# Moving intermediates of two delta-rule mixers from SBUF to PSUM, two copies' engine and one subtraction's place

## The chip, the cores and the metric

The program runs on one core of a Trainium2 chip. The time is that of the whole program in device microseconds (us), the median of three runs. One core has five engines that run side by side, each through its own list of instructions in order: TensorE (PE, matrix products), VectorE (DVE), ScalarE (ACT), GpSimd (POOL) and SyncE (SP, which here only issues DMAs).

## The reference

Two blocks of a sequence model are applied to 512 tokens of 1024 features. The first block has two layers; each is a mixer and a feed-forward part. The change touches the two mixers of this block alone. What they compute, cut to the parts that matter:

```python
qkv = jax.nn.silu(centred_depthwise_conv(jnp.concatenate([qd, kd, vd], axis=-1), dn_conv_w[l]))  # 5 taps
qd = l2norm(qd...) * DN_DK ** -0.5 ; kd = l2norm(kd...)
...
gcum = jnp.cumsum(g, axis=-1)                      # g: log decay; chunks of 64 tokens, 8 heads
decay = jnp.exp(jnp.where(incl, gcum[..., :, None] - gcum[..., None, :], -jnp.inf))
a_kk = jnp.where(strict, jnp.einsum("bhnid,bhnjd->bhnij", k_beta, k) * decay, 0.0)
t_inv = lax.linalg.triangular_solve(eye + a_kk, ...)           # 64x64 unit lower triangles
qk = jnp.einsum("bhnid,bhnjd->bhnij", q, k) * decay
q_dec = q * jnp.exp(gcum)[..., None]
...
def step(state, inp): ...                          # a scan over the 8 chunks, both directions
```

Beside this delta rule each mixer has a softmax attention over the same tokens (queries and keys normalised per head and turned by a rotary table), and gates that mix the two branches.

## The kernel before

The activations lie in SBUF with features on partitions: a tile is 128 features x 512 tokens, one PSUM bank. A projection is 8 pieces of contraction times three matmuls of 512 columns (high x high, high x low, low x high parts of float32), 24 matmuls; the weights come by DMA (`wraw`, issued by SP), are rounded to a high part by ACT (`whi`, line 478), and POOL subtracts to get the low part (`wlo`, line 384, which is the line of a helper `tt` and so of most two-tensor operations).

A mixer (`_mix`) runs in this order. First come eight tiles of keys and queries, each through `conv_tile`: a projection, a product with the row norms into `pad` (line 384), ACT's first tap (line 701), four taps of DVE (line 703) and a SiLU (lines 516 and 517). `l2` normalises them: squares, transposes and sums, a Newton root on DVE (lines 394 to 400), the roots spread into `rce` (line 453, in `spread`), transposed on PE and multiplied into the tiles (line 733). Then `inside` goes through four pairs of heads and two directions, eight steps. A step takes two exponentials on ACT (lines 847 and 853) and on DVE and POOL: the decayed keys (line 849, `s<-kq,eg`), the decayed queries (POOL, `s<-kq,eg`), a subtraction (POOL), a minimum with the mask (DVE, `x<-x,cstt`), the product with the query-key matrix (DVE, `s<-kkqq,x`), the one with beta (POOL) and the one with the key-key matrix (DVE, `x<-x,kkqq`). The results go to DRAM. Beside `inside` run `vproj` (four convolution tiles of values, `cv`) and `zproj` (four tiles `z`). After that the key-key matrices are read back as `N`, and `solve` inverts all triangles on DVE: for j = 1 to 30 a product into `ntmp` and a sum into `N`. Beside the solve run the attention's keys and queries and some gates; `core`, the attention itself, starts before the solve has ended: scores (line 955), maxima (line 959), exponentials, transposes, the two parts `pT` and `pTl`, and the product with the values (line 974) into a bank from `psg`. Last come the scan over the chunks and the output projections.

PSUM has eight banks. Two are always kept for projections (`psb`); `self.banks(3, 3)` gives the first stage of a mixer three of kind `pss` and three of kind `psf`; the solve and the attention have `banks(2, 3, 1)`, one of them of kind `psg`. A buffer of a pool is given again only when the last use of what it held is over.

The order of each engine's list is set by a scheduler, which goes by its own simulated times; generators with costs (`side.beside(inside(), R1)`) only set the order in which the program is written.

Of the kernel before, what the change touches and what calls it, by code (L numbers as in the profile page):

```python
# [305 lines left out]
class Prog:  # L306
# [139 lines left out]
    def spread(self, rc, wide=None, nt=4, psum=None):  # L446


        nc = self.nc
        if wide is not None:  # L450
            e = self.nrm.tile([P, 4, P], F32, name="rce", tag="nsq", bufs=2)
            for a, b in wide(e, rc):
                nc.vector.tensor_copy(a, b)
            col = lambda t: e[:, t]
        else:
            col = lambda t: rc[:, t].broadcast_to((P, P))
        ps = (psum or self.pss)()
        for t in range(nt):
            nc.tensor.transpose(ps[:, t * P:(t + 1) * P], col(t), self.ident)
        return ps  # L460
# [187 lines left out]
    def _mix(self, l, nm, nxt, mp):  # L648
# [30 lines left out]
        mt = mid.enter_context(tc.tile_pool(name="mid", bufs=1))  # L679
        th = lambda name="th", bufs=3: mt.tile([P, S], F32, name=name, tag=name, bufs=bufs)  # L680
        bk = ExitStack()
        bk.enter_context(self.banks(3, 3))
        reg = ExitStack()
        r1 = reg.enter_context(tc.tile_pool(name="mr1", bufs=1))
        cs = lambda name, bufs=2, shape=(P, S): r1.tile(list(shape), F32, name=name, tag=name, bufs=bufs)
# [5 lines left out]
        npad = [0]  # L691


        def conv_tile(i, w, c):
            ps = self.psb()
            self.proj(ps, w, nm.acts)
            u = pads[npad[0] % 2]
            npad[0] += 1
            self.tt(u[:, 2:S + 2], ps, nm.r, ALU.mult)
            tap = lambda k: self.vec(f"cw{l}", i * 5 + k)  # L700
            nc.scalar.activation(c, u[:, 2:S + 2], AF.Copy, scale=tap(2))
            for k in (0, 1, 3, 4):
                nc.vector.scalar_tensor_tensor(c, u[:, k:k + S], tap(k), c, ALU.mult, ALU.add)
            return c

        kq = []

        def qk_pair(g, first, a):
            ws = self.wload(win[g], 8, 256)
            for j in range(2):  # L710
                if a == 0:
                    kq.append(kv("kq", (first + j) // 2))
                c = kq[first + j][:, a]
                conv_tile(first + j + 4 * (1 - a), ws[j], c)
                self.silu2(c, c, th())


        wide2 = lambda e, a: [(e.rearrange("p t (h d) -> p t h d", h=2), a.unsqueeze(3).broadcast_to((P, 4, 2, 64)))]
# [92 lines left out]
        def vproj():  # L811
            for g in range(4, 6):
                ws = self.wload(win[g], 8, 256)
                for j in range(2):
                    p = 2 * (g - 4) + j
                    c = conv_tile(8 + p, ws[j], th("cv", 2))
                    t = th()
                    self.silu2(c, c, t)
                    by_chunk(vst[:, :, p], c, self.psf(), 0.5)
                    yield 6  # L820

# [4 lines left out]
        def inside():  # L826
            for p in range(4):
                kT, qT = kq[p][:, 0], kq[p][:, 1]
                kb, km = kbds[p % 2], kkqq[p % 2].rearrange("p a (c k x) -> p (a c) k x", c=4, k=2)
                for h in range(2):  # L830
                    sl = slice(h * 64, h * 64 + 64)
                    nc.scalar.copy(kb[sl, :, sl], c8(kT)[sl])
                for b in range(2):
                    ps = self.pss()
                    for c in range(4):
                        sl = slice((4 * b + c) * 64, (4 * b + c) * 64 + 64)
                        nc.tensor.matmul(ps[:, c * P:(c + 1) * P], kb[:, 4 * b + c], kq[p][:, :, sl], start=True, stop=True)
                    nc.scalar.copy(kkqq[p % 2][:, b], ps)
                kk, qq = km[:, :, 0], km[:, :, 1]
                kt = cs("kt")  # L840
                by_chunk(c8(kt), kT, self.pss(), 1.0)
                nc.sync.dma_start(out=scrK[:, p].rearrange("q c x -> q (c x)"), in_=kt)
                for d in (1, 0):
                    u0 = (d * 4 + p) * 8
                    gr = grs[2 * p + 1 - d]
                    eg = cs("eg")
                    nc.scalar.activation(eg, gr, AF.Exp)
                    s3 = cs("s3", 2, (P, 3, S))
                    nc.vector.scalar_tensor_tensor(s3[:, KE], kT, -1.0, eg, ALU.mult, ALU.mult)
                    self.tt(s3[:, QD], qT, eg, ALU.mult, "gpsimd")  # L850
                    self.tt(c8(gr), c8(gr), gc[:, u0:u0 + 8].unsqueeze(2).broadcast_to((P, 8, 64)), ALU.subtract, "gpsimd")
                    self.tt(c8(gr), c8(gr), mask[d].unsqueeze(1).broadcast_to((P, 8, 64)), ALU.min)
                    nc.scalar.activation(gr, gr, AF.Exp)
                    self.tt(c8(s3[:, QK]), qq, c8(gr), ALU.mult)
                    for h, a in enumerate(half):
                        nc.sync.dma_start(out=dn[d, a, p, 0:h + 2:h + 1].rearrange("q k c x -> q k (c x)"), in_=s3[a, 0:2])
                        nc.sync.dma_start(out=dn[d, half[1 - h], p, 1 + h].rearrange("q c x -> q (c x)"), in_=s3[a, QK])
                    self.tt(c8(gr), c8(gr), nbeta[:, u0:u0 + 8].unsqueeze(2).broadcast_to((P, 8, 64)), ALU.mult, "gpsimd")
                    self.tt(c8(gr), c8(gr), kk, ALU.mult)
                    if d == 0:  # L860
                        nc.sync.dma_start(out=scrN[:, p].rearrange("c q x -> q c x"), in_=c8(gr))
                    else:
                        ps = self.pss()
                        for t in range(4):
                            nc.tensor.transpose(ps[:, t * P:(t + 1) * P], gr[:, t * P:(t + 1) * P], self.ident)
                        nt = cs("nt")
                        nc.scalar.copy(nt, ps)
                        for c2 in range(2):
                            nc.sync.dma_start(out=scrT[:, c2:8:2, p], in_=nt[c2 * 64:c2 * 64 + 64].rearrange("i (t y) -> i t y", t=4))
                    yield 8  # L870
# [46 lines left out]
        def queries(g):  # L917
# [7 lines left out]
            rq[g] = self.rs_cols([sq for _, sq in qs], four, 2, 1.0, 64 * EPS, psum=self.psf, r=nm)  # L925
            for q, _ in qs:
                turn(q)
                for h in range(2):
                    t = at.tile([P, S], F32R, name="qa", tag="qa", bufs=5)
                    qa.append(t)  # L930
                    nc.scalar.copy(t, q)
                    for o in (0, 64):
                        a, b = slice(o + h * 32, o + h * 32 + 32), slice(o + 32 - h * 32, o + 64 - h * 32)
                        self.tt(t[b], q[a], t[a].bitcast(F32), ALU.subtract, "gpsimd")
            yield 2

        pv_last = []
# [78 lines left out]


        def solve(sp):
            tmp = sp.tile([P, 1024], F32, name="ntmp")
            Nm = N[:, :4096].rearrange("p (j i) -> p j i", j=64)  # L1020
            nc.sync.dma_start(out=Nm[64:128], in_=scrT.rearrange("j c p (h i) -> (c p h) j i", h=2))
            nc.sync.dma_start(out=Nm[0:64], in_=scrN.rearrange("c p (h j) i -> (c p h) j i", h=2))
# [2 lines left out]
            Nh = N.rearrange("p (a x) -> p a x", a=2)[:, :, :2048].rearrange("p a (j i) -> p a j i", i=64)  # L1025
            for j in range(1, 31):
                n = 31 - j
                t = tmp[:, :2 * j * n].rearrange("p (a c i) -> p a c i", a=2, c=j)
                self.tt(t, Nh[:, :, 0:j, j:j + 1].broadcast_to((P, 2, j, n)),
                        Nh[:, :, j:j + 1, j + 1:32].broadcast_to((P, 2, j, n)), ALU.mult)  # L1030
                self.tt(Nh[:, :, 0:j, j + 1:32], Nh[:, :, 0:j, j + 1:32], t, ALU.add)
# [771 lines left out]
```

## Time and profile before

| | |
|---|---|
| median of 3 runs | 3408.35 us (3406.65 to 3415.18) |
| the profiled execution | 3408.12 us, span from first to last instruction 3406.3 us |
| PE busy | 3214.2 us, 94% of the span |
| DVE, POOL, ACT busy | 1917.2 us (56%), 1810.2 us (53%), 1486.5 us (44%) |

A busy share is a mean over the whole program. The two mixers lie near 13 to 490 us and 936 to 1365 us, the rest is feed-forward parts, and another block. A row of a view has the line of the program, the engine, the operation, the tile written and the tiles read, the shapes, and times.

### The profile page before, as it was taken

How to read it: one execution, taken by the hardware profiler on the slowest of the kernel's cores; microseconds unless marked ns; L12 is line 12 of the kernel's file. 1: busy time of each engine (PE TensorE's matmuls, PEld its weight loads, DVE VectorE, ACT ScalarE, POOL GpSimd, SP SyncE). 2: the span in 40 equal slices, each digit the busy share in tenths (PEclk: the TensorE clock that was granted, in tenths of full speed). 3: DMA queues.
4: the chain of work that ended last, by engine and by line, in shares of the span. 5: the costliest groups of instructions: out<-in, count | busy, mean ns of one | idle time of the engine just before them, and what ended most of it. 6: DMA issues, size and time to landing. Idle time of an engine off the chain costs nothing. (4 is left out here: it accounts for less than half of the span.)

```text
span 3406.3 us, 46975 instructions
## 1 busy us (share of the span) xinstructions
PE 3214.2 (94%) x17342; PEld 2649.1 (78%) x17342; DVE 1917.2 (56%) x3561; ACT 1486.5 (44%) x2776; POOL 1810.2 (53%) x1493
## 2 busy tenths in 40 slices
PE   8878899999987889999999998999999999999999
PEld 6667778888776667788887787878888888888887
DVE  8988555554698866573455665463223666453222
ACT  4636434343554553443343335544334455544332
POOL 4653465444565434654455556555556335655554
PEclk9989999999998999999999999999999999999999
DMA  4532532222354234322232213233223213222222
GB/s 145 166 90 62 132 117 99 96 90 96 122 155 126 71 92 132 133 93 94 99 113 75 75 47 127 87 125 122 95 99 108 82 65 118 99 87 99 99 99 87
DMA packets 140477, 350.93 MB, mean 103 GB/s; under 512 B 43567, under 2 KB 80815, under 8 KB 111576
## 3 DMA queue, kind: packets, MB, share of 16 engines
q1 hardware_dynamic: 138816, 344.44, 31.4%
q10 hardware_dynamic: 1432, 3.49, 0.4%
q8 instruction: 138, 2.26, 0.3%
q14 instruction: 91, 0.75, 0.1%
HBM read 316.34 MB, written 34.16 MB: 103 GB/s over the span
## 5 line engine op out<-in xcount | busy, mean ns | idle before, releaser
L384 POOL TENSOR_TENSOR wlo<-wraw,whi 128x512 fp32r<-128x512 f32 (+2 forms) x1044 | 1372.0, 1318 | 1363.9 <-ACT whi L478 1333.9
L478 ACT CAST whi<-wraw 128x512 fp32r<-128x512 f32 (+2 forms) x1044 | 631.6, 608 | 1111.7 <-PE psb L494 846.6
L491 PE MATMUL psb<-act,whi 128*128 128x512 f32 x1888 | 756.6, 401 | 50.8 <-DVE x L384 15.5
L494 PE MATMUL psb<-act,whi 128*128 128x512 f32 x1888 | 750.8, 398 | 0.6 <-DVE act L277 0.6
L495 PE MATMUL psb<-act,wlo 128*128 128x512 f32 x1888 | 749.3, 398 | 1.7 <-POOL wlo L384 1.6
L491 PEld LDWEIGHTS psb<-act,whi 128*128 128x128 f32 x1888 | 361.9, 192 | 130.3 <-issue 34.1
L495 PEld LDWEIGHTS psb<-act,wlo 128*128 128x128 f32 x1888 | 361.4, 191 | 79.1 <-POOL wlo L384 3.7
L494 PEld LDWEIGHTS psb<-act,whi 128*128 128x128 f32 x1888 | 361.9, 192 | 74.4 <-DVE act L277 2.0
L384 DVE TENSOR_TENSOR x<-psb,x 128x512 f32<-128x512 f32 x168 | 115.2, 689 | 381.3 <-PE psb L495 381.0
L491 PE MATMUL ps<-act,whi 128*128 128x512 f32 (+1 forms) x720 | 282.5, 392 | 3.4 <-ACT rB L303 3.4
L494 PE MATMUL ps<-act,whi 128*128 128x512 f32 (+1 forms) x720 | 281.6, 391 | 0.0
L495 PE MATMUL ps<-act,wlo 128*128 128x512 f32 (+1 forms) x720 | 281.6, 391 | 0.0
L491 PE MATMUL psb<-mid,whi 128*128 128x512 f32 x704 | 276.7, 394 | 1.0 <-DVE x L384 1.0
L495 PE MATMUL psb<-mid,wlo 128*128 128x512 f32 x704 | 276.2, 392 | 0.0
L494 PE MATMUL psb<-mid,whi 128*128 128x512 f32 x704 | 273.6, 389 | 0.0
L491 PEld LDWEIGHTS ps<-act,whi 128*128 128x128 f32 (+1 forms) x720 | 134.9, 187 | 34.4 <-ACT rB L303 4.9
L495 PEld LDWEIGHTS ps<-act,wlo 128*128 128x128 f32 (+1 forms) x720 | 134.7, 187 | 29.9
L494 PEld LDWEIGHTS ps<-act,whi 128*128 128x128 f32 (+1 forms) x720 | 135.0, 188 | 29.4
L495 PEld LDWEIGHTS psb<-mid,wlo 128*128 128x128 f32 x704 | 132.2, 188 | 30.5
L494 PEld LDWEIGHTS psb<-mid,whi 128*128 128x128 f32 x704 | 132.1, 188 | 29.5
L491 PEld LDWEIGHTS psb<-mid,whi 128*128 128x128 f32 x704 | 132.3, 188 | 29.3 <-DVE x L384 1.5
L384 DVE TENSOR_TENSOR cv<-ps,cv 128x512 f32<-128x512 f32 (+1 forms) x60 | 41.5, 692 | 174.6 <-PE ps L495 106.8
(434 smaller groups left out, 5584.8 us busy)
## 6 DMA issues: line engine op xcount, KB each, us to landing
wraw<-in_wup SPq DMA_DIRECT2D x44, 1024.0 KB, 4.8
wraw<-in_fup SPq DMA_DIRECT2D x44, 1024.0 KB, 4.8
wraw<-in_win SPq DMA_DIRECT2D x38, 1024.0 KB, 5.0
wraw<-in_wdn SPq DMA_DIRECT2D x16, 1024.0 KB, 4.8
wraw<-in_evin SPq DMA_DIRECT2D x16, 1024.0 KB, 4.8
wraw<-in_xakv SPq DMA_DIRECT2D x16, 1024.0 KB, 4.8
wraw<-in_fdn SPq DMA_DIRECT2D x16, 1024.0 KB, 4.8
wraw<-in_odin SPq DMA_DIRECT2D x12, 1024.0 KB, 4.9
```

What stands on the lines that cost most here:

```text
L384: getattr(self.nc, eng).tensor_tensor(out, a, b, op)
L478: nc.scalar.copy(hi, part)
L491: mm = nc.tensor.matmul(ps, hi[:, i], acts[k][:, 0, :n], start=k == 0, stop=False)
L494: nc.tensor.matmul(ps, hi[:, i], acts[k][:, 1, :n], start=False, stop=False)
L495: nc.tensor.matmul(ps, lo[:, i], acts[k][:, 0, :n], start=False, stop=k == kc - 1)
```

## The change

Five edits, all in the two mixers:

- the four DVE taps of `conv_tile` accumulate in a PSUM bank (`psg`), and the SiLU's last operation writes the result to SBUF; the first stage's banks become `(2, 2, 2)`;
- both exponentials of an `inside` step are written to PSUM banks of kind `psf` (`eg`, `en`); the decayed queries move from POOL to DVE; beta is multiplied into the key-key matrix (`kb`, still POOL) ahead of the decay instead of after it;
- the copies that spread roots (`rce`) go from DVE to ACT;
- in `queries`, POOL's four subtractions of 32 partitions for each pair of heads' low parts, eight for each of the two groups of queries, become one of 128 partitions to `lo`, followed by four DMAs on SP;
- the solve's product goes to a PSUM bank `pt`, the one bank of kind `psg`, instead of SBUF; `ntmp` stays for a later layout step.

```diff
@@ spread
-                nc.vector.tensor_copy(a, b)
+                nc.scalar.copy(a, b)
@@ _mix
-        bk.enter_context(self.banks(3, 3))
+        bk.enter_context(self.banks(2, 2, 2))
@@ conv_tile
-        def conv_tile(i, w, c):
-            ps = self.psb()
+        def conv_tile(i, w, out):
+            ps, c = self.psb(), self.psg()
...
                 nc.vector.scalar_tensor_tensor(c, u[:, k:k + S], tap(k), c, ALU.mult, ALU.add)
-            return c
+            self.silu2(c, out, th())
@@ inside
-                    eg = cs("eg")
+                    eg = self.psf()
                     nc.scalar.activation(eg, gr, AF.Exp)
                     s3 = cs("s3", 2, (P, 3, S))
                     nc.vector.scalar_tensor_tensor(s3[:, KE], kT, -1.0, eg, ALU.mult, ALU.mult)
-                    self.tt(s3[:, QD], qT, eg, ALU.mult, "gpsimd")
+                    self.tt(s3[:, QD], qT, eg, ALU.mult)
...
-                    nc.scalar.activation(gr, gr, AF.Exp)
-                    self.tt(c8(s3[:, QK]), qq, c8(gr), ALU.mult)
+                    en = self.psf()
+                    nc.scalar.activation(en, gr, AF.Exp)
+                    self.tt(c8(s3[:, QK]), qq, c8(en), ALU.mult)
...
-                    self.tt(c8(gr), c8(gr), nbeta[:, u0:u0 + 8].unsqueeze(2).broadcast_to((P, 8, 64)), ALU.mult, "gpsimd")
-                    self.tt(c8(gr), c8(gr), kk, ALU.mult)
+                    kb = cs("eg")
+                    self.tt(c8(kb), kk, nbeta[:, u0:u0 + 8].unsqueeze(2).broadcast_to((P, 8, 64)), ALU.mult, "gpsimd")
+                    self.tt(c8(gr), c8(en), c8(kb), ALU.mult)
@@ queries
+                lo = th("cv", 2)
+                self.tt(lo, q, ts[0].bitcast(F32), ALU.subtract, "gpsimd")
+                for h, t in enumerate(ts):
                     for o in (0, 64):
                         a, b = slice(o + h * 32, o + h * 32 + 32), slice(o + 32 - h * 32, o + 64 - h * 32)
-                        self.tt(t[b], q[a], t[a].bitcast(F32), ALU.subtract, "gpsimd")
+                        nc.sync.dma_start(out=t[b].bitcast(F32), in_=lo[a])
@@ solve
-            tmp = sp.tile([P, 1024], F32, name="ntmp")
+            tmp, pt = sp.tile([P, 1024], F32, name="ntmp"), self.psg()
...
-                t = tmp[:, :2 * j * n].rearrange("p (a c i) -> p a c i", a=2, c=j)
+                t = pt[:, :2 * j * n].rearrange("p (a c i) -> p a c i", a=2, c=j)
```

The lists move at three places. The first is DVE's list where `inside` begins in the first mixer. Before, the first decayed keys (`s_881`, `s_967`) stand among the convolution taps and ahead of the second normalisation, whose sums begin at the last row:

```order
L453 COPY rce<-rc 128x512
L703 SCALAR_TENSOR_TENSOR cv<-pad_227,vect,cv 128x512
L849 SCALAR_TENSOR_TENSOR s_881<-kq,eg 128x512
L849 SCALAR_TENSOR_TENSOR s_967<-kq,eg 128x512
L384 TENSOR_TENSOR pad_228<-psb,rB 128x512
L703 SCALAR_TENSOR_TENSOR cv<-pad_228,vect,cv 128x512
L733 SCALAR_TENSOR_TENSOR kq<-kq,ps_587 128x512
L733 SCALAR_TENSOR_TENSOR kq<-kq,ps_595 128x512
L703 SCALAR_TENSOR_TENSOR cv<-pad_228,vect,cv 128x512
L384 TENSOR_TENSOR x<-x,cstt 128x512
L420 TENSOR_REDUCE sums<-ps_779 128x8
```

Now the same place in the program has all taps (`ps_1173` is the last convolution's bank) and the whole second normalisation in front; the first decayed keys are `s_889`:

```order
L703 SCALAR_TENSOR_TENSOR ps_1173<-pad_228,vect,ps_1173 128x512
L398 SCALAR_TENSOR_TENSOR rsq<-rsq,ps_811 128x32
L384 TENSOR_TENSOR rsq<-rsq,ps_811 128x32
L400 SCALAR_TENSOR_TENSOR rc<-rsq,ps_811 128x32
L731 SCALAR_TENSOR_TENSOR kq<-kq,ps_832 128x512
L731 SCALAR_TENSOR_TENSOR kq<-kq,ps_840 128x512
L731 SCALAR_TENSOR_TENSOR kq<-kq,ps_848 128x512
L731 SCALAR_TENSOR_TENSOR kq<-kq,ps_856 128x512
L846 SCALAR_TENSOR_TENSOR s_889<-kq,ps_887 128x512
L384 TENSOR_TENSOR s_889<-kq,ps_887 128x512
L384 TENSOR_TENSOR x<-x,cstt 128x512
```

The eight steps of `inside` have moved behind the second normalisation, whose banks are of the same kind as theirs.

The second place is the end of the solve on DVE in the first mixer. Before, six values of `pTl` stand further ahead among the solve's sums (not shown), and the seventh behind the last sum:

```order
L384 TENSOR_TENSOR N<-N,ntmp 128x2x29x2
L384 TENSOR_TENSOR ntmp<-N 128x60
L959 TENSOR_REDUCE mx<-ps_2253 128x1
L384 TENSOR_TENSOR N<-N,ntmp 128x2x30
L384 TENSOR_TENSOR mx<-mx,rc 128x1
L1042 COPY ntmp<-N 64x1024
L384 TENSOR_TENSOR pTl<-ps_2118,pT 128x4x128
L959 TENSOR_REDUCE mx<-ps_2268 128x1
```

Now, with `ps_1520` the bank of the products and `ps_1943` the first bank of the attention's output:

```order
L384 TENSOR_TENSOR ps_1520<-N 128x60
L384 TENSOR_TENSOR mx<-mx,rc 128x1 x2
L384 TENSOR_TENSOR N<-N,ps_1520 128x2x30
L1044 COPY ntmp<-N 64x1024
L384 TENSOR_TENSOR pTl<-ps_2083,pT 128x4x128
L384 TENSOR_TENSOR pTl<-ps_2126,pT 128x4x128
L384 TENSOR_TENSOR cv<-ps_1943,cv 64x512
L1045 COPY N<-N 64x32x32
L384 TENSOR_TENSOR pTl<-ps_2151,pT 128x4x128
L384 TENSOR_TENSOR pTl<-ps_2166,pT 128x4x128
```

Only four values of `pTl` now stand ahead of the last sum, and the next ones and the first output of the attention (`cv<-ps_1943`) follow behind it.

The third place is SP's list between the reading of `N` and the writing of the inverses (`ti`). Before:

```order
L1022 DMA N<-scrN 64x4096
L1021 DMA N<-scrT 64x64x64
L465 DMA wraw<-in_win 128x2048 x6
L1048 DMA ti_196<-N 16x4096
```

Now:

```order
L1024 DMA N<-scrN 64x4096
L868 DMA scrT<-nt 256x1x128 x2
L1023 DMA N<-scrT 64x64x64
L465 DMA wraw<-in_win 128x2048 x2
L936 DMA qa<-cv 32x512 x4
L465 DMA wraw<-in_win 128x2048
L936 DMA qa<-cv 32x512 x4
L465 DMA wraw<-in_win 128x2048 x2
```

Three of the weight fetches stand behind DMAs that wait for POOL's `lo` (in a tile named `cv`).

## Rows read from the trace of the kernel before

**Rows 1.** Busy time by stretch: first mixer thrice, a feed-forward part, second mixer's solve.

```profile
core 0: us, PE busy (x) PEld busy (x) DVE busy (x) ACT busy (x) POOL busy (x), PEclk, DMA share, GB/s
29.00:167.40 138.40, 120.03 (x616) 97.00 (x617) 130.44 (x176) 76.09 (x144) 82.05 (x56) 0.96 0.48 141
186.30:267.60 81.30, 68.20 (x296) 55.06 (x297) 79.68 (x136) 31.99 (x63) 42.80 (x28) 0.90 0.19 67
267.60:345.00 77.40, 65.94 (x372) 52.20 (x372) 61.37 (x116) 50.02 (x102) 28.17 (x20) 1.00 0.22 55
595.00:680.00 85.00, 85.00 (x375) 70.06 (x375) 44.08 (x48) 31.96 (x52) 42.09 (x32) 1.00 0.26 92
1064.50:1145.10 80.60, 68.92 (x296) 55.60 (x297) 79.44 (x136) 32.03 (x63) 42.37 (x28) 0.88 0.20 70
```

**Rows 2.** Timeline near 148 us, DVE and POOL: start, us, engine, line.

```profile
146.78 3.41 POOL L384 TENSOR_TENSOR wlo<-wraw,whi 128x512 fp32r<-128x512 f32 x2
147.29 1.75 DVE L703 SCALAR_TENSOR_TENSOR cv<-pad,vect,cv 128x512 f32<-128x512 f32 x1
148.97 1.77 DVE L384 TENSOR_TENSOR x<-x,kkqq 128x512 f32<-128x512 f32 x1
```

**Rows 3.** Instructions on tile pad: count, shortest/median/longest ns, first and last start.

```profile
L384 DVE TENSOR_TENSOR pad<-psb,rB x112: 675/686/694, 29.0 to 3363.8; 128x512 f32<-128x512 f32 x112
L703 DVE SCALAR_TENSOR_TENSOR kq<-pad,vect,kq x64: 730/752/1830, 30.5 to 965.1; 128x512 f32<-128x512 f32 x64
```

**Rows 4.** Groups of instructions by line and form: busy us, mean ns, idle before.

```profile
L703 DVE SCALAR_TENSOR_TENSOR kq<-pad,vect,kq 128x512 f32<-128x512 f32 x64 | 63.8, 1010 | 5.9 <-ACT kq L701 5.3
L384 POOL TENSOR_TENSOR qa<-th,qa 32x512 fp32r<-32x512 f32 x32 | 47.7, 1492 | 9.4 <-ACT qa L931 4.0 <-issue 3.6
L703 DVE SCALAR_TENSOR_TENSOR cv<-pad,vect,cv 128x512 f32<-128x512 f32 x32 | 33.2, 1041 | 2.1 <-ACT cv L701 1.6
L849 DVE SCALAR_TENSOR_TENSOR s<-kq,eg 128x512 f32<-128x512 f32 x16 | 26.8, 1694 | 0.0
L384 DVE TENSOR_TENSOR x<-x,kkqq 128x512 f32<-128x512 f32 x16 | 24.1, 1528 | 0.0
L384 DVE TENSOR_TENSOR x<-x,cstt 128x512 f32<-128x512 f32 x16 | 15.9, 997 | 2.6 <-POOL x L384 2.6
L453 DVE COPY rce<-rc 128x512 f32<-128x512 f32 x16 | 12.9, 825 | 0.0
L847 ACT ACTIVATE eg<-x 128x512 f32<-128x512 f32 x16 | 10.1, 632 | 28.8 <-POOL s L384 11.0 <-DVE s L849 10.6 <-DMA x<-scrG 5.0
```

**Rows 5.** Instructions on tile kq, two of DVE's, in the columns of rows 3.

```profile
L517 DVE SCALAR_TENSOR_TENSOR kq<-th,kq x16: 673/692/1692, 38.5 to 966.6; 128x512 f32<-128x512 f32 x16
L733 DVE SCALAR_TENSOR_TENSOR kq<-kq,ps x16: 672/675/680, 89.9 to 1014.4; 128x512 f32<-128x512 f32 x16
```

**Rows 6.** Timeline of DVE: first decayed keys, second normalisation's copies, last key-key products.

```profile
93.99 1.76 DVE L849 SCALAR_TENSOR_TENSOR s<-kq,eg 128x512 f32<-128x512 f32 x1
...
123.43 2.45 DVE L453 COPY rce<-rc 128x512 f32<-128x512 f32 x2
...
165.03 2.37 DVE L384 TENSOR_TENSOR x<-x,kkqq 128x512 f32<-128x512 f32 x2
```

**Rows 7.** The solve's two groups, all forms together, in both mixers.

```profile
L384 DVE TENSOR_TENSOR ntmp<-N 128x60 f32<-128x60 f32 (+14 forms) x60 | 49.3, 822 | 16.2 <-DMA N<-scrT 15.4
L384 DVE TENSOR_TENSOR N<-N,ntmp 128x60 f32<-128x60 f32 (+14 forms) x60 | 40.7, 679 | 0.5
```

**Rows 8.** Two of the solve's fifteen sizes by themselves, both mixers.

```profile
L384 DVE TENSOR_TENSOR N<-N,ntmp 128x440 f32<-128x440 f32 x4 | 2.4, 611 | 0.1
L384 DVE TENSOR_TENSOR N<-N,ntmp 128x60 f32<-128x60 f32 x4 | 0.9, 232 | 0.0
```

**Rows 9.** What PE waited for: total us, times, longest.

```profile
PE psb L491 <- DVE N L384: 12.0, 2, 6.3
PE psb L491 <- ACT whi L478: 9.8, 1, 9.8
PE ps L955 <- DVE rc L384: 7.2, 2, 3.6
```

**Rows 10.** A DMA issue of SP from 80 to 200 us: count, size, us to landing.

```profile
dnscr<-s SPq DMA_DIRECT2D x16, 128.0 KB, 4.7
```

More of the change, by code (lines that the diff above doesn't have):

```diff
@@ L712, in qk_pair @@
                     kq.append(kv("kq", (first + j) // 2))
-                c = kq[first + j][:, a]
-                conv_tile(first + j + 4 * (1 - a), ws[j], c)
-                self.silu2(c, c, th())
+                conv_tile(first + j + 4 * (1 - a), ws[j], kq[first + j][:, a])
         wide2 = lambda e, a: [(e.rearrange("p t (h d) -> p t h d", h=2), a.unsqueeze(3).broadcast_to((P, 4, 2, 64)))]
@@ L815, in vproj @@
                     p = 2 * (g - 4) + j
-                    c = conv_tile(8 + p, ws[j], th("cv", 2))
-                    t = th()
-                    self.silu2(c, c, t)
+                    c = th("cv", 2)
+                    conv_tile(8 + p, ws[j], c)
                     by_chunk(vst[:, :, p], c, self.psf(), 0.5)
@@ L828, in inside @@
                 kT, qT = kq[p][:, 0], kq[p][:, 1]
-                kb, km = kbds[p % 2], kkqq[p % 2].rearrange("p a (c k x) -> p (a c) k x", c=4, k=2)
+                kbd, km = kbds[p % 2], kkqq[p % 2].rearrange("p a (c k x) -> p (a c) k x", c=4, k=2)
                 for h in range(2):
                     sl = slice(h * 64, h * 64 + 64)
-                    nc.scalar.copy(kb[sl, :, sl], c8(kT)[sl])
+                    nc.scalar.copy(kbd[sl, :, sl], c8(kT)[sl])
                 for b in range(2):
@@ L836, in inside @@
                         sl = slice((4 * b + c) * 64, (4 * b + c) * 64 + 64)
-                        nc.tensor.matmul(ps[:, c * P:(c + 1) * P], kb[:, 4 * b + c], kq[p][:, :, sl], start=True, stop=True)
+                        nc.tensor.matmul(ps[:, c * P:(c + 1) * P], kbd[:, 4 * b + c], kq[p][:, :, sl], start=True, stop=True)
                     nc.scalar.copy(kkqq[p % 2][:, b], ps)
@@ L927, in queries @@
                 turn(q)
-                for h in range(2):
-                    t = at.tile([P, S], F32R, name="qa", tag="qa", bufs=5)
-                    qa.append(t)
+                ts = [at.tile([P, S], F32R, name="qa", tag="qa", bufs=5) for h in range(2)]
+                qa.extend(ts)
+                for t in ts:
                     nc.scalar.copy(t, q)
+                lo = th("cv", 2)
+                self.tt(lo, q, ts[0].bitcast(F32), ALU.subtract, "gpsimd")
+                for h, t in enumerate(ts):
                     for o in (0, 64):
                         a, b = slice(o + h * 32, o + h * 32 + 32), slice(o + 32 - h * 32, o + 64 - h * 32)
-                        self.tt(t[b], q[a], t[a].bitcast(F32), ALU.subtract, "gpsimd")
+                        nc.sync.dma_start(out=t[b].bitcast(F32), in_=lo[a])
             yield 2
```

## Prediction

> **What bounds the kernel now.** I read the busy time by stretch first. In a feed-forward part PE is busy all of 85 us and issues 375 matmuls, one every 0.227 us [rows 1]; nothing that the other engines do faster can help there, and the change does not touch it. The mixers are different. From 29.0 to 167.4 us, the convolutions and `inside`, DVE is busy 130.4 of 138.4 us; from 186.3 to 267.6, the solve, 79.7 of 81.3, and in the second mixer the solve's stretch looks the same [rows 1]. The granted clock there is 0.96 and 0.90; PE stands still in between. So DVE sets the pace of these two stretches, and what it saves there can be seen in the end. Between them lies a DMA round trip, behind them the attention, where DVE has 61.4 of 77.4 us [rows 1] and nothing is saturated.
>
> The timeline tells why DVE is so full. Near 148 us one operation with two SBUF inputs takes 1.75 us, the next 1.77, while POOL works without a gap [rows 2]. The same tap elsewhere takes 0.730 at least and 0.752 in the middle, 1.830 at most; the product `pad<-psb,rB`, which reads one input from PSUM, runs 0.675 to 0.694 in all 112 cases [rows 3]. A DVE operation with both inputs in SBUF waits for POOL, one with an input in PSUM does not.
>
> **The change part by part**, for one mixer (rows that cover both are halved).
>
> Taps: 96 take 97.0 us [rows 4]. At 0.752 they take 72.2, so 12.4 us less per mixer. The decayed keys: 16 at 1.694; at 0.675, what `kq<-kq,ps` takes [rows 5], 8.0 less. The decayed queries come to DVE: eight at 0.675, 5.4 more. The key-key products: 1.528 to 0.675, 6.8 less. The eight copies of roots, 0.825 each, leave: 6.6 less [rows 4]; ACT, busy 76.1 of 138.4 us, has room for eight at about 0.63. Together DVE has 28 us less of its 130.
>
> No row shows an operation that writes 512 columns to PSUM and reads them back. Both ends: the row with PSUM input costs 0.675 against 0.673 for the shortest with SBUF alone [rows 5], so nothing; or the 0.079 us by which a tap exceeds it [rows 3, 5], on 122 operations of a mixer (48 taps, 12 SiLUs, 32 in `inside`, 30 sums) 9.6 us. I take nothing, since only the first row differs in the memory alone. [...]
>
> But the 28 us don't all shorten the stretch, because of the order. The two exponentials of a step now need banks of kind `psf`, which the second normalisation and `by_chunk` use as well; the order shows all eight steps behind that normalisation, where four decayed keys stood ahead of its root. So I place two points. The second normalisation's copies start at 123.4 us now [rows 6]. Of DVE's work ahead of them, 40 taps lose 10.3 us, the first copies leave 3.3, and four decayed keys, four minima, four query-key products (0.675 each) and two key-key products move behind, by rows 4 about 16.5: DVE would be there at 93.3. PE has 312 projection matmuls from 29.0 to that point, 70.8 us at 0.227, so not before 99.8; with 64 small transposes and the wait for the first normalisation I take 108. From there run eight steps. A step in which each waits for the one before is two exponentials at 0.632 [rows 4], four DVE operations at 0.675 and a minimum at 0.997, 4.96 us, and about one of a convolution's or `z`'s operations: 6.0. Eight end at 156, where 167.4 stands now (165.03 and 2.37 [rows 6]): 11 us earlier. The bounds of a step are 4.7, DVE's work alone, and 9.2, the pace now ((167.4 - 93.99) / 8): from 21 earlier to 14 later.
>
> The stretch of the round trip, 18.9 us to 186.3, I leave as it is.
>
> The solve: 60 sums take 40.7 us, 60 products 49.3 [rows 7]. From sizes 60 and 440 at 0.232 and 0.611 [rows 8] an operation alone is 0.172 us plus 0.997 per thousand elements; a solve has 30 sums with 9,920 elements, 15.1 us against 20.35: 5.3 less. The products still read both inputs from SBUF; only their output is in PSUM. I count no direct gain for them; bounds are 0 and 9.6 less. POOL has less to do: of its 42.8 us in this stretch [rows 1] eight of the 32-partition subtractions at 1.49 [rows 4] go, 11.9, and two of about 1.3 come. That is 22% less work of POOL's; of the 9.6 us that the products wait, 2.1 go. One copy of roots and one of sums go to ACT, 0.9. Together 8 us less, on an engine that stands idle for 1.6 us in this stretch: 8 us.
>
> [...] No row here shows an operation with two SBUF inputs and PSUM output. [...]
>
> What comes back: the solve's product holds the only `psg` bank, which the attention's output needs. Now six of 32 score tiles are through `pTl` before the solve's last sum; in the new order four are, and no product with the values. The next stretch takes 77.4 / 26 = 3.0 us a tile. Two tiles later at half that price, since their scores and maxima are done, is 3 us; bounds 0 and 6.
>
> The DMAs: sixteen per mixer on SP, each landing about 4.7 us after issue if it is like a 128 KB store [rows 10]. With 1.3 for the subtraction that is 6.0, where four of POOL's took 4 x 1.49 = 6.0. I cost them at nothing: PE waits at the scores for the root `rc`, not for `qa` [rows 9]. Weight fetches stand behind them on SP, but PE waited for weights only once, at the start [rows 9]; with that cover gone, one late fetch costs about a landing, 4.7 us.
>
> The 6 us twice that PE waited behind DVE's wait for `N` [rows 9] go, as `cv<-psb` now stands ahead of it; PE was not the pace there, so nothing.
>
> Sum for a mixer: 11 + 8 - 3 = 16; for both 32. From the profiled execution's 3408.1 us (span 3406.3 and 1.8 around it; it equals the median of 3408.35 within 0.3): 3376.
>
> **The rivals.** First, DVE's saving lands nearly whole: steps at 4.7 us and products relieved too. Then 21 + 8 + 8 - 3 = 34 a mixer, 3340 (the products' 9.6 less the 2.1 counted already are the second 8). For it: filler operations can cover the exponentials. Against it: the banks' order.
>
> Second, slower: two `psf` banks for `eg`, `en`, the values' transposes and, before them, the roots make each step wait for the release of the one before, and ACT, in order, holds exponentials behind weight rounding. At today's 9.2 us a step, `inside` ends 14 later: 14 - 8 + 3 = 9 a mixer, 3426. It decides from 8.1 us a step, where 108 + 8 x 8.1 = 173 eats the solve's 5 net.
>
> Third, given back: behind the solve, attention needs all six tiles again at 3.0 us, 18, so 11 + 8 - 18 = 1 a mixer, 3406. For it: PE and the chain of score, exponential and transpose set that stretch, not DVE. Against: maxima are taken ahead as before.
>
> Fourth, the change doesn't do what it says: reading and writing PSUM costs the 0.079 us, 9.6 a mixer. 16 - 9.6 = 6.4, 3395.
>
> **How the numbers follow.** Forecast 0.50, first rival 0.17, second 0.12, third 0.15, fourth 0.06. The forecast's own range is 3364 to 3387 (steps of 5.3 to 6.7 us). 8 in 10 reach from 3340 to 3408: below lies half of the first rival, above the second. A measurement tells about 0.3%, 10 us, from no change. Faster by more (below 3398): 0.48 of the forecast, 0.17 and 0.04 of the fourth, 0.69. Within: 0.02 of the forecast, 0.01 of the second, 0.13 of the third, 0.02 of the fourth, 0.18. Slower: 0.11 of the second and 0.02 of the third, 0.13.
>
> **What would show it.** Taps near 0.75 us in every case and no more of 1.75; decayed keys near 0.7; sums of the solve near 15 us a mixer, products still uneven; the last key-key product near 156; a solve stretch near 73 us; the first product with the values right behind the last sum; PE's clock with fewer falls. The forecast is wrong if `inside` shows DVE idle between steps waiting for ACT, if PE waits for weights near the query DMAs, or if the attention stretch grows by more than 6 us.

## The result, and the profile after

The changed kernel takes 3364.97 us (median of 4 runs, 3362.22 to 3368.71) against 3407.5 (4 runs, 3406.32 to 3415.18) for the kernel before beside it: a ratio of 0.9877, 95% interval 0.9865 to 0.9889. It is 42.5 us faster, where 32 were forecast. The profiled execution has a span of 3362.7 us, 43.6 less than before.

Busy time by stretch of the changed kernel, with the columns of [rows 1]; the ends of the stretches are the first decayed keys, the last key-key product, the solve's first product, its last sum and the last product with the values, and the last row is the second mixer's solve:

```profile
core 0: us, PE busy (x) PEld busy (x) DVE busy (x) ACT busy (x) POOL busy (x), PEclk, DMA share, GB/s
29.00:114.30 85.30, 83.72 (x435) 67.80 (x435) 66.01 (x127) 49.62 (x88) 35.59 (x28) 1.00 0.34 105
114.30:159.70 45.40, 39.39 (x201) 33.57 (x202) 36.67 (x51) 34.30 (x70) 26.50 (x23) 0.89 0.79 219
159.70:183.80 24.10, 19.72 (x87) 15.74 (x86) 7.68 (x21) 6.75 (x13) 8.94 (x7) 0.93 0.92 204
183.80:248.40 64.60, 53.31 (x235) 42.02 (x233) 63.10 (x129) 26.72 (x53) 27.00 (x20) 0.94 0.24 82
248.40:325.90 77.50, 68.56 (x393) 56.45 (x394) 59.85 (x112) 53.57 (x109) 18.12 (x13) 0.98 0.24 62
1040.20:1105.40 65.20, 52.67 (x226) 41.20 (x224) 63.04 (x127) 26.29 (x53) 27.86 (x20) 0.92 0.24 82
```

Up to the last key-key product, DVE is busy 102.7 of 130.7 us, where it was 130.4 of 138.4. Ahead of the steps it is PE that has no time left, 83.7 of 85.3. The solve takes 64.6 us instead of 81.3, the attention 77.5 as before (77.7: its last product with the values ends at 345.4, 0.4 us behind the end of the row in [rows 1]).

The groups that answer to [rows 3], [rows 4] and [rows 7] (for the first line: count, shortest/median/longest ns, first and last start; for the others busy us, mean ns, idle before):

```profile
L703 DVE SCALAR_TENSOR_TENSOR ps<-pad,vect,ps x96: 734/756/756, 30.6 to 963.2; 128x512 f32<-128x512 f32 x96
```

```profile
L846 DVE SCALAR_TENSOR_TENSOR s<-kq,ps 128x512 f32<-128x512 f32 x16 | 11.0, 688 | 10.7 <-ACT ps L844 8.7 <-DMA dnscr<-s 2.0
L384 DVE TENSOR_TENSOR x<-ps,eg 128x512 f32<-128x512 f32 x16 | 10.9, 684 | 0.6 <-POOL eg L384 0.6
L384 DVE TENSOR_TENSOR x<-x,cstt 128x512 f32<-128x512 f32 x16 | 18.5, 1155 | 1.6 <-POOL x L384 1.6
L384 DVE TENSOR_TENSOR ps<-N 128x60 f32<-128x60 f32 (+14 forms) x60 | 43.1, 718 | 12.3 <-DMA N<-scrT 11.5
L384 DVE TENSOR_TENSOR N<-N,ps 128x60 f32<-128x60 f32 (+14 forms) x60 | 29.6, 494 | 0.7
```

All 96 taps now lie between 734 and 756 ns, where the longest took 1830; decayed keys went from 1694 to 688, key-key products from 1528 to 684, the solve's sums from 679 to 494. What still has two SBUF inputs remains long: the minimum `x<-x,cstt` takes 1155 ns in the mean, the solve's products 718.

The new limit ahead of the steps stands in DVE's timeline before the first decayed keys (start, us, engine, line, and in brackets the idle time and its releaser):

```profile
105.50 0.19 DVE L400 SCALAR_TENSOR_TENSOR rc<-rsq,ps 128x32 f32<-128x32 f32 x1
111.30 1.29 DVE L731 SCALAR_TENSOR_TENSOR kq<-kq,ps 128x512 f32<-128x512 f32 x2 [5.61 <-PE ps L459]
112.80 1.29 DVE L731 SCALAR_TENSOR_TENSOR kq<-kq,ps 128x512 f32<-128x512 f32 x2 [0.21 <-PE ps L459]
114.29 0.69 DVE L846 SCALAR_TENSOR_TENSOR s<-kq,ps 128x512 f32<-128x512 f32 x1 [0.21 <-ACT ps L844]
```

DVE has the roots of the second normalisation ready at 105.7, but waits 5.6 us for PE to spread them. ACT has copied the first half of them by 107.4; PE is busy with projections until its first spreading matmul starts at 110.7. Between the last key-key product and the solve lies the round trip. SP's issues in the changed kernel, and its wait for the last read:

```profile
160.51 0.54 SPq L860 DMA_DIRECT2D scrN<-x  x1
161.14 0.65 SPq L465 DMA_DIRECT2D wraw<-in_win  x1
164.64 0.47 SPq L1024 DMA_DIRECT2D N<-scrN  x1
165.20 1.21 SPq L868 DMA_DIRECT2D scrT<-nt  x2
174.47 0.60 SPq L1023 DMA_DIRECT2D N<-scrT  x1
SPq L1023 <- DMA scrT<-nt: 8.0, 1, 8.0
```

And in the kernel before:

```profile
169.33 1.19 SPq L869 DMA_DIRECT2D scrT<-nt  x2
170.61 0.58 SPq L1022 DMA_DIRECT2D N<-scrN  x1
172.41 0.60 SPq L1021 DMA_DIRECT2D N<-scrT  x1
SPq L1021 <- DMA scrT<-nt: 1.1, 1, 1.1
```

The last read of N is issued 14.8 us after the last key-key product; in the kernel before it was 5.0 after it. It waits for the two stores of `nt`, which now stand behind the first read of N in SP's list and land 8.8 us after their issue instead of 2.4. In the second mixer the stores stand ahead of the read as before, and the trip is still 3.1 us longer, so the order is not the whole of it.

### The profile page after: what moved, and what is told of

The parts are those of the page before. It is cut to its first block, busy times and chain, and to the rows that moved or that the text cites. A ratio compares the mean times of both kernels' runs of the same rounds, so it can differ in the third digit from the quotient of the medians.

```text
span 3362.7 us, 47054 instructions
## 1 busy us (share of the span) xinstructions
PE 3198.5 (95%) x17342; PEld 2643.8 (79%) x17342; DVE 1832.8 (55%) x3549; ACT 1499.9 (45%) x2804; POOL 1719.1 (51%) x1453
## 5 line engine op out<-in xcount | busy, mean ns | idle before, releaser
L384 POOL TENSOR_TENSOR wlo<-wraw,whi 128x512 fp32r<-128x512 f32 (+2 forms) x1044 | 1353.1, 1299 | 1420.8 <-ACT whi L478 1382.6
```

The source lines that it names most:

```text
L384: getattr(self.nc, eng).tensor_tensor(out, a, b, op)
```

## The experiments

The theory was the forecast's: a DVE operation with both inputs in SBUF is lengthened by POOL's work (a tap took up to 1.830 us [rows 3]), one with an input in PSUM isn't (0.694 at most [rows 3]), and DVE sets the pace up to the solve's end. The rivals: waits for PSUM banks eat the saving; POOL's smaller load alone explains the solve; PE is the next limit. Five of the twelve runs undo one edit, one makes one edit alone, and the others move or take away work or banks. With each edit the scheduler orders the lists anew, so what a run shows is the edit together with its order. Ratios are to the kernel before on the same chip; the changed kernel has 0.9877.

**Products of the solve back in SBUF.**

```diff
-                t = pt[:, :2 * j * n]...
+                t = tmp[:, :2 * j * n]...
```

> The changed kernel with the solve's products back in SBUF, all else as changed. If an operation waits for POOL only where both inputs lie in SBUF, the 30 sums of a mixer lengthen from 14.9 us towards 20.3; as POOL has 27.0 us in that stretch instead of 42.8, the excess is about 5.2 x 27.0 / 42.8 = 3.3, the products stay near 21.6, and the time is 3365 + 7 = 3372. If the output's memory counts as well, the products return towards 24.2 and it is 3365 + 12 = 3377. If the solve was quicker only because POOL has less to do and work moved ahead of N, the sums stay below 16 and it is 3365.

Measured: 3376.96 us, ratio 0.9916 (0.9902 to 0.9930), so the edit is worth some 13 us. Solve and attention of the first mixer:

```profile
183.20:256.60 73.40, 62.71 (x275) 49.66 (x274) 72.07 (x133) 29.77 (x60) 28.07 (x20) 0.92 0.22 73
256.60:329.90 73.30, 64.06 (x361) 52.10 (x359) 58.20 (x108) 50.28 (x103) 19.24 (x14) 0.98 0.26 65
```

```profile
L384 DVE TENSOR_TENSOR ntmp<-N 128x60 f32<-128x60 f32 (+14 forms) x60 | 46.6, 777 | 9.1 <-issue 4.6 <-DMA N<-scrT 3.6
L384 DVE TENSOR_TENSOR N<-N,ntmp 128x60 f32<-128x60 f32 (+14 forms) x60 | 37.8, 630 | 0.4
```

The sums grow from 29.6 to 37.8 us for both mixers, 18.9 a mixer. The excess of the kernel before, 20.35 - 14.8, scaled by POOL's busy time in the solve (28.1 of 42.8 us), gives 18.4. The products grow by 59 ns each with nearly the same load on POOL, 1.8 us a mixer. The single instructions tell why: of the 60 products of both mixers, those with no POOL operation beside them keep to 0.172 us plus 0.997 per thousand elements within 0.02 us with the output in PSUM (29 in the changed kernel) and within 0.06 with it in SBUF (34 here). POOL works beside 21.0 us of them in the changed kernel and beside 24.1 us here. So it is the time beside POOL that differs, not the output's memory. The solve is 8.8 us longer, but the attention 4.2 shorter, as the output's bank is free and products with the values start at 234 instead of 248 us.

**Queries' low parts by POOL again.**

```diff
-                lo = th("cv", 2)
-                self.tt(lo, q, ts[0].bitcast(F32), ALU.subtract, "gpsimd")
...
-                        nc.sync.dma_start(out=t[b].bitcast(F32), in_=lo[a])
+                        self.tt(t[b], q[a], t[a].bitcast(F32), ALU.subtract, "gpsimd")
```

> The changed kernel with the queries' low parts again as 32-partition subtractions on POOL and no DMAs, all else as changed. By the forecast's term the solve's products lengthen by about 2 us a mixer, and nothing else changes: 3365 + 4 = 3369. If POOL's smaller load is what doubled the solve's gain (8.7 us a mixer over the forecast), the solve's stretch grows from 64.6 to about 73, and it is 3365 + 17 = 3382. If the DMAs cost something, as SP stands in front of other transfers, it falls below 3365.

Measured: 3380.87 us, ratio 0.9924 (0.9910 to 0.9938), so this edit is worth 16 us.

```profile
183.20:250.50 67.30, 54.01 (x236) 42.12 (x234) 66.36 (x129) 27.05 (x53) 37.11 (x26) 0.95 0.20 72
250.50:330.50 80.00, 69.32 (x393) 56.50 (x394) 59.81 (x112) 53.74 (x109) 26.57 (x19) 0.98 0.21 53
```

```profile
L384 DVE TENSOR_TENSOR ps<-N 128x60 f32<-128x60 f32 (+14 forms) x60 | 48.1, 801 | 13.1 <-DMA N<-scrT 12.4
L384 DVE TENSOR_TENSOR N<-N,ps 128x60 f32<-128x60 f32 (+14 forms) x60 | 29.8, 496 | 0.7
```

With POOL busy 37.1 us in the solve instead of 27.0, the products, with two SBUF inputs, go from 718 to 801 ns, and the sums, with one, stay at 496. That is 2.5 us a mixer, near the forecast's 2.1. But POOL is also 8.5 us busier in the attention, which is 2.5 us longer: there another 2.5 us of the edit's worth lie. In the second mixer the steps and the round trip are longer too (by 1.7 and 3.1 us), far from the edit's work; the experiment doesn't say why. The time is the 3382 of the expectation's second case, but not for its reason: the solve's stretch grows to 67.3 us and not to 73.

**Decays in SBUF, decayed queries on POOL.**

```diff
-                    eg = self.psf()
+                    eg = cs("eg")
...
-                    self.tt(s3[:, QD], qT, eg, ALU.mult)
+                    self.tt(s3[:, QD], qT, eg, ALU.mult, "gpsimd")
...
-                    en = self.psf()
-                    nc.scalar.activation(en, gr, AF.Exp)
+                    nc.scalar.activation(gr, gr, AF.Exp)
...
```

Beta is multiplied in behind the decay again, as in the kernel before.

> The changed kernel with the decay exponentials back in SBUF and the decayed queries back on POOL (beta order as before), convolutions, solve, queries and roots as changed. DVE's work in the eight steps of a mixer grows by 8.0 for the keys and 6.8 for the products and loses 5.4 for the queries, 9.4 us; DVE had 8.7 us idle in that stretch. If DVE sets the pace there, about two thirds of it return: 3365 + 12 = 3377. If the wait for two PSUM banks costs as much as the faster operations save, the steps start ahead of the second normalisation again and nothing changes: 3365. If the banks cost more than that, it is below 3362.

Measured: 3363.6 us, ratio 0.9872 (0.9858 to 0.9887): the edit is worth nothing here.

```profile
29.00:85.90 56.90, 56.90 (x290) 45.42 (x291) 47.44 (x88) 32.70 (x58) 24.59 (x20) 1.00 0.36 112
85.90:159.50 73.60, 67.96 (x366) 55.96 (x365) 62.50 (x83) 50.73 (x101) 56.46 (x41) 1.00 0.62 185
```

```profile
L846 DVE SCALAR_TENSOR_TENSOR s<-kq,eg 128x512 f32<-128x512 f32 x16 | 25.9, 1649 | 1.2 <-DMA dnscr<-s 1.2
```

The decayed keys take 1649 ns again. The first decayed keys come at 85.9 instead of 114.3, the eight steps take 73.6 us instead of 45.4, and the last key-key product ends at 159.5, as in the changed kernel. DVE has 7 us more to do and finds room for it; PE is busy 124.9 of 130.5 us.

**Convolution sums in SBUF, and this edit alone.** In the first, all else is as changed; in the second, all else is as before.

```diff
-            ps, c = self.psb(), self.psg()
+            ps, c = self.psb(), out
```

> The changed kernel with the convolution sums back in SBUF, all else as changed. The 48 taps of a mixer lengthen from 0.76 to about 1.0 us, 12 us of DVE's time, 8 of them ahead of the eight steps and 4 beside them. If DVE sets the pace in both, they come back nearly whole: 3365 + 20 = 3385. If PE, busy for 83.7 of the 85.3 us ahead of the steps, sets it there, only the 4 beside the steps can show: 3365 + 8 = 3373 at most, and DVE's idle time ahead of the steps shrinks from 19 to 11 us.

> The kernel before with one edit of the change alone: the convolution sums in PSUM, with the banks that need it; decay exponentials, solve, queries and roots as before. If the convolutions carry the earlier end of the eight steps by themselves, the last key-key product ends near 160 instead of 167.4 and the time is 3405 - 15 to 20 = 3387. If DVE needs the decays' saving as well (its work there falls by 12 of 130 us only), the last product ends near 165 and it is 3400.

Measured: without the edit 3387.65 us, ratio 0.9948 (0.9935 to 0.9960); the edit alone 3382.72, ratio 0.9932 (0.9919 to 0.9944). Either way it is worth 23 to 24 us, the most of all. The taps without the edit:

```profile
L703 DVE SCALAR_TENSOR_TENSOR kq<-pad,vect,kq 128x512 f32<-128x512 f32 x64 | 66.3, 1050 | 5.4 <-ACT kq L701 4.6
L703 DVE SCALAR_TENSOR_TENSOR cv<-pad,vect,cv 128x512 f32<-128x512 f32 x32 | 27.7, 864 | 9.1 <-ACT cv L701 8.7
```

Without it, the last key-key product ends at 167.8, where the kernel before had 167.4: the other edits do nothing for that point. The expectation's "3373 at most" was wrong. The first decayed keys do come at 114.7, as with PE as the pace, but the steps take 53.1 us instead of 45.4: eight taps, 6.8 us of DVE's work, now stand among them, where the changed kernel has none. With the edit alone, the last key-key product ends at 162.4, 5 us earlier, and 14 us earlier in the second mixer, of which 10 had been gained by the end of the first mixer's scan (431.8 us instead of 441.8). Part of that is order: the first solve's stretch is 7.2 us shorter, though its sums and products together are no faster (46.0 against 44.6 us), as DVE now does 13.4 us of work in the round trip instead of 4.5.

**Fewer matmuls for PE, in both kernels.** The 32 low-part matmuls of a mixer's four value convolutions are left out, so that the values are less exact. The diff is the same for both.

```diff
...
-                nc.tensor.matmul(ps, lo[:, i], acts[k][:, 0, :n], start=False, stop=k == kc - 1)
+                if low:
+                    nc.tensor.matmul(ps, lo[:, i], acts[k][:, 0, :n], start=False, stop=k == kc - 1)
...
-            self.proj(ps, w, nm.acts)
+            self.proj(ps, w, nm.acts, low=i < 8)
```

> The changed kernel without the low-part matmuls of the four value convolutions of each mixer: 32 of PE's products of 128x512 a mixer are left out (7.3 us at 0.227), the values are less exact, DVE, ACT and POOL do the same. If PE sets the pace from 29 to 160 us in the changed kernel, the eight steps end about 7 us earlier in each mixer, and the time is 3365 - 14 = 3351. If DVE or the chain of a step sets it, nothing changes: 3365.

> The kernel before without the same 32 matmuls a mixer (the low parts of the value convolutions' weights are left out). If DVE sets the pace there, as the forecast read it, nothing changes: 3405. If PE set it there already, it is 3405 - 14 = 3391.

Measured: 3347.61 us, ratio 0.9829 (0.9815 to 0.9842), from the changed kernel, 16 us less; 3399.5, ratio 0.9981 (0.9972 to 0.9989), from the kernel before, 6.5 us less. Here is the first mixer of the changed kernel without them:

```profile
29.00:108.40 79.40, 76.71 (x403) 61.69 (x403) 65.78 (x127) 49.42 (x88) 35.64 (x28) 1.00 0.38 119
108.40:153.30 44.90, 41.60 (x216) 35.87 (x217) 36.33 (x51) 33.81 (x71) 25.59 (x23) 0.92 0.76 212
```

All 32 leave the stretch ahead of the first step (403 matmuls there instead of 435), and 5.9 of their 7.3 us are gained there: PE sets the pace to 114 us. The steps lost none of PE's work and keep their 45 us, so this run says nothing of their pace; the run on z below does. In the kernel before, the steps end 2.1 us earlier, the round trip takes that back, and the end of the first solve comes forward by 0.7 us, from 267.7 to 267.0: there DVE did set the pace in the main. The attention is then 2.4 us shorter, the second mixer's attention ends 3.3 us earlier, and the rest of the 6.5 lies behind the mixers. The expected 3405 was missed by as much, and no run shows why the attention is shorter.

**Other banks for solve and attention.**

```diff
-        bk.enter_context(self.banks(2, 3, 1))
+        bk.enter_context(self.banks(2, 2, 2))
```

> The changed kernel with two banks of the attention output's kind and two instead of three for scores in the solve and attention stretches, so that the solve's products and the attention's output have a bank each; nothing else. If the wait for that bank costs the attention stretch the 4 us by which it is shorter with the products in SBUF, products with the values run ahead of the last sum again and the time is 3365 - 8 = 3357, less what the third score bank was worth. If the score bank matters more, the attention stretch grows beyond 78 us and it is over 3365.

Measured: 3382.21 us, ratio 0.9929 (0.9915 to 0.9942), 17 us slower than the changed kernel. Products with the values start at 231 us again, but the attention stretch grows to 86.0 us:

```profile
183.00:247.00 64.00, 54.49 (x245) 43.92 (x243) 60.50 (x122) 25.96 (x50) 25.70 (x19) 0.92 0.23 82
247.00:333.00 86.00, 70.50 (x382) 55.64 (x382) 62.58 (x120) 55.75 (x114) 19.49 (x14) 0.96 0.22 56
```

The third score bank is worth more than a bank of its own for the output: the stretch grows by 8.5 us (7.0 in the second mixer), although the output has its own bank.

**PE's z projections moved behind the steps**, with decays as changed and with decays in SBUF.

```diff
-        side = Side(vproj(), zproj(), islice(gates, G1))
+        zp = zproj()
+        side = Side(vproj(), islice(zp, 0))
...
-        side = Side(merge(heads, islice(gates, G2)), gates)
+        side = Side(merge(heads, islice(gates, G2)), zp, gates)
```

> The changed kernel with the four projections of z of each mixer taken from beside the eight steps to beside the solve, so that 96 of PE's products (22 us) leave the stretch up to the last key-key product and gate projections follow later; nothing else. If PE sets that stretch, the last product ends earlier until DVE, busy 103 of 131 us less 6 for z, or the chain of a step sets it: near 148 instead of 160. PE has 33 us idle between 29 and 326 us, 24 of them in the round trip, the solve and the attention, so part of it comes back there; the time is 3365 - 6 to 16 = 3354. If the chain of the steps sets it, the last product stays near 160 and z lengthens the solve by 1.4 us a tile: 3365 + 11 = 3376.

> The changed kernel with the same move of the z projections, and with the decay exponentials in SBUF and the decayed queries on POOL as before the change. If the decays in PSUM were worth nothing because PE set the stretch, they must show here: DVE has 9.4 us more to do in it, and the last product ends 5 to 9 us later than with the move alone. If waits for the PSUM banks eat what they save, it ends as early as there, or earlier.

Measured: 3403.37 us, ratio 0.9999 (0.9990 to 1.0009), and with the decays in SBUF 3391.93, ratio 0.9963 (0.9951 to 0.9975). Both lose against the changed kernel, and the expected 3354 was wrong: the first mixer's scan ends at 420 us instead of 422, but the second mixer's first decayed keys come at 989 instead of 973. The projections of z now run beside the solve, and the gates' projections that stood there move on: from the first step to the end of the first attention PE issues 819 matmuls instead of 914. Those put off are paid for in full, as PE is busy 483.6 of the 484.7 us from the scan's end to 905 us and nothing can hide them there. The pair still tells what it was made for. What DVE waited for between 114 and 161 us, with the decays in PSUM (total us, times, longest; the three longest totals):

```profile
DVE s L846 <- DMA dnscr<-s: 6.4, 2, 4.9
DVE s L846 <- ACT ps L844: 5.6, 6, 1.4
DVE s L384 <- ACT ps L851: 2.2, 2, 1.2
```

```profile
114.10:160.60 46.50, 32.64 (x164) 27.41 (x164) 30.76 (x44) 30.07 (x64) 22.80 (x20) 0.86 0.77 218
```

The first decayed keys stand at 114.1, as in the changed kernel, and the last key-key product at 160.6, though PE is busy for 32.6 us there instead of 39.4 and DVE for 30.8 instead of 36.7: so neither engine sets the pace there, but the chain within the steps. In six steps DVE waits for ACT's first exponential, twice for the second, and twice for the DMAs that empty `s3`. With the decays in SBUF, the steps start at 86.0 and end at 154.2, 6.4 us earlier, and the kernel is 11 us faster than its sister. This is the second case of the expectation: here the edit costs time. Argued from the order, and not tried by itself: behind the second normalisation, eight steps in a row have less to cover their waits.

**Root copies on DVE.**

```diff
-                nc.scalar.copy(a, b)
+                nc.vector.tensor_copy(a, b)
```

> The changed kernel with the copies that lay out the roots back on DVE, all else as changed. With PE as the pace up to 160 us, the 6.6 us a mixer of these copies on DVE fit into its idle time there and the time is 3365 to 3367; two copies of the solve's stretch add 0.9 us a mixer. If the copies sit on the path to the second normalisation, each of four adds 0.2 us (0.83 against 0.63): also under 3368. By the forecast's sum, where all of DVE's work counts, it is 3365 + 13 = 3378.

Measured: 3363.66 us, ratio 0.9880 (0.9867 to 0.9892): worth nothing, as expected with PE as the pace.

**Three banks for the decays, one for the convolution sums.**

```diff
-        bk.enter_context(self.banks(2, 2, 2))
+        bk.enter_context(self.banks(2, 3, 1))
         reg = ExitStack()
         r1 = reg.enter_context(tc.tile_pool(name="mr1", bufs=1))
```

> The changed kernel with three banks instead of two of the kind that the decay exponentials, the roots and the values' transposes use, and one instead of two for the convolution sums, from the convolutions to the eight steps; nothing else. If two banks make each step wait for the one before (5.7 us a step, which stayed when 22 us of PE's work were taken away), steps shorten towards DVE's own 4.7, the last key-key product ends 5 to 8 us earlier, and the time is 3365 - 8 = 3357, since part of it returns in the round trip. If the chain of exponential, subtraction, minimum and exponential over three engines sets the step, it stays at 5.7 us and the time is 3365. If a single bank for the sums holds up PE ahead of the steps, the first decayed key stands later than 114.3 and the time is above 3368.

Measured: 3360.63 us, ratio 0.9868 (0.9847 to 0.9889), not to be told from the changed kernel; the profiled execution took 3372.6. The first decayed keys come at 109.3, and the steps take 46.6 us. What DVE waited for in the steps, from 109 to 156:

```profile
DVE s L846 <- DMA dnscr<-s: 4.9, 1, 4.9
DVE s L846 <- ACT ps L844: 3.3, 3, 1.7
DVE s L384 <- ACT ps L851: 1.5, 2, 1.0
```

The same rows in the changed kernel, from 114 to 161:

```profile
DVE s L846 <- ACT ps L844: 3.6, 6, 1.4
DVE s L846 <- DMA dnscr<-s: 2.0, 1, 2.0
DVE s L384 <- ACT ps L851: 0.9, 1, 0.9
```

With three banks the waits for the exponentials are 4.8 us together, with two 4.5, and the wait for the emptied `s3` grows from 2.0 to 4.9. So the number of banks is not what holds the steps. Whether the stores do, with more banks, is not shown: more buffers for `s3` were not tried. No version that does all the work is faster than the changed kernel beyond the measurement.

## Why the prediction was right, and where its terms were off

By undoing, convolution sums are worth 24 us, the queries' low parts 16, the solve's products 13, decays and roots nothing. That is 53 for a whole of 42.5. Each is known to some 6 us, so the excess of 11 is about what the intervals together allow, and whether the edits depend on each other is not shown. Each was measured with the others present, and only the convolutions were also tried alone.

**The mechanism** held. DVE operations lost their lengthening wherever an input moved to PSUM (the longest tap fell from 1830 to 756 ns, the decayed keys from 1694 to 688 in the mean), those that kept two SBUF inputs stayed exposed to POOL (the products took 718 ns with POOL busy for 27.0 us of the solve, 801 with 37.1), and the time fell where DVE set the pace. That reading and writing PSUM costs next to nothing was right too for what was measured: a tap takes 0.756 us in the middle against 0.752, and a sum of 440 columns 608 ns against 611, 4 ns more and 3 less. With that the fourth rival, 79 ns an operation, falls. That the products gain nothing directly from their output in PSUM was the author's estimate, with no row of the kernel before to show it; the run with them back in SBUF showed 59 ns more each, with POOL beside them for 24.1 us instead of 21.0, and those without POOL beside them on the same line either way.

The total came out better than its terms: the steps were forecast 3.3 us too high, round trip and solve 3.5 too low and the attention's charge of 3 did not show. That the first two errors cancel is luck. The time lies at the lower end of the forecast's own range, 3364 to 3387.

**Steps of `inside`, 11 forecast, 7.7 measured** (8.0 in the second mixer). The sum placed the second normalisation's end at 108; it was 114.3. The forecast made PE the limit there, rightly, but took 99.8 us plus eight for small matmuls and a wait; all 435 matmuls kept PE busy for 83.7 us, the 123 small ones for about 13. The step was sized well: 45.4 / 8 = 5.7 us against 6.0. What the forecast had as a saving of three edits is that of one. The convolutions took the pace from DVE and gave it to PE, and what decays and roots save on DVE behind that is idle time. One of the forecast's signs of being wrong did show in part: DVE idles 4.5 us of the steps' 45.4 for ACT's exponentials. Of the second rival the order is real: with z moved, the steps in a row behind the second normalisation end 6.4 us later than those with decays in SBUF. Its cause, two banks, is not: with three the steps took 46.6 us. Its price, 9.2 us a step, was too high.

**Round trip and solve, 8 forecast, 11.5 measured** (12.3 in the second). The parts were off more than the sum: the solve lost 16.7 us, the round trip grew by 5.2 (3.1 in the second). The sums' 5.3 is 5.6, the products' 2.1 is 3.1. The failed step is the work that crosses the ends of the solve, which the forecast put at nothing for the solve. Behind its end go two values of `pTl` and one output of the attention, 2.0 us of DVE's work; the forecast charged 3 us for the tiles to the attention, but did not take their work off the solve, where DVE sets the pace. Ahead of its start, and larger, four operations of the attention's keys and values move into the round trip, where DVE is busy 7.7 us instead of 4.5, and one of 0.7 us into the steps; the forecast left the round trip as it was. With sums and products that makes some 14 of the 16.7; the rest is mostly other operations that got shorter, such as the low part of the values, `va<-th,va`, from 1.79 to 0.69 us. The round trip's growth belongs to SP's order more than to one edit: it took 19.2 us with the decays in SBUF, but 21.3 with the convolutions' edit alone and 17.9 with z moved.

**Attention, 3 more forecast, nothing measured.** The charge was right and is 4: with the products in SBUF the stretch takes 73.3 us. The forecast missed that POOL's relief by the queries' edit, 2.5 us there, comes off in that stretch as well; and the stretch of before, with the bank free but the old queries, was 77.7. What cancels the other 1.7 us of the charge is not shown. The third rival falls.

**Query DMAs at nothing**: no wait of PE, DVE or ACT for them shows, they land 2.0 us after issue where 4.7 were taken, and the edit pays.

In all, 16 a mixer were forecast and 19.4 and 20.7 measured by the ends of the two scans, besides some 3.5 us behind them.

## What to carry to other kernels

Ask after each edit of a change, and not only before the first, which engine sets the pace of a stretch: here the convolutions' edit handed it to PE ahead of the steps, and two of the other four were worth nothing. Work that an order moves across a stretch's end must be entered twice, as a charge where it goes and as a saving where it leaves. The PSUM bank that `banks(2, 2, 2)` gave to one use was taken from another in `banks(2, 3, 1)`, and the price is read at the other's stretch: a score bank less made the attention 7 to 8.5 us a mixer longer, although it freed a bank whose lack costs 4.

## What the runs showed of the hardware

Accumulating in place in PSUM cost DVE 4 ns a tap more than in SBUF: 0.756 us against 0.752, the shortest 0.734 against 0.730. What POOL's work added to the solve's sums on two SBUF inputs fell with that work: the 30 sums of a mixer take 20.4 us with POOL busy for 42.8 us of the stretch, 18.9 with 28.1, and 14.8 to 14.9 with one input in PSUM, whether POOL is busy for 27.0 or 37.1. The single instructions show it without means: in the kernel before, the 33 of 60 sums with no POOL operation beside them keep to 0.172 us plus 0.997 per thousand elements within 0.03 us, and the others exceed it by up to 0.98; in the changed kernel 22 sums run beside POOL for nearly all their time, and none of the 60 exceeds it by more than 0.02. An output in PSUM didn't spare the products: with two SBUF inputs they still took 718 ns in the mean, where the sums of the same sizes took 494, and 801 with the busier POOL.
